# A kernel of two transformer blocks: the compression's weights move past its blocks, keys and values side by side, the gates' columns beside the first values'

## The chip, the cores and the metric

One core of one Trainium2 chip runs the whole program. The metric is device time in microseconds (us), as the median of three runs. Times in the trace are microseconds from the first instruction; the profiled execution is one execution by itself.

## The reference

Two blocks are computed on 512 tokens of width 1024 in f32. The change lies in the first one, in its mixer:

```python
h = rmsnorm(x, norm_mix_pre[i])
z = h @ w_in[i]
xr, gr, q, kc, vc, ksl, vsl, kw, vw, g_nsa, gm_rnn, gm_attn = jnp.split(z, IN_SPLITS, axis=-1)
...
kc_c = compress(kc.reshape(kv_shape), cmp_pos_k[i], cmp_k_w1[i], cmp_k_w2[i])
vc_c = compress(vc.reshape(kv_shape), cmp_pos_v[i], cmp_v_w1[i], cmp_v_w2[i])
y_attn = nsa(q, kc_c, vc_c, ksl..., vsl..., kw..., vw..., g_nsa, slopes)

def compress(kv, pos, w1, w2):          # kv: [1, 512, 4 groups, 64]
    c = kv.reshape(B, S // 16, 16, G, dh)
    blk = jnp.concatenate([c[:, :-1], c[:, 1:]], axis=2)   # 31 blocks of 32 tokens
    blk = blk + pos[:, None, :]
    blk = blk.transpose(0, 1, 3, 2, 4).reshape(B, nc, G, 32 * dh)   # 2048 wide
    return jax.nn.gelu(blk @ w1) @ w2    # w1: [2048, 256], w2: [256, 64]
```

`g_nsa` are 48 gate columns (16 heads by three branches) that go through a sigmoid; `vsl` and `vw` are 256 value columns each of the selected and the window branch. After the mixer come an output projection, a feed-forward stage, and a second block with a mixture of experts; none of that is touched.

## The kernel before

The program is written in a framework that records instructions with their data dependencies and then orders them by a planner of its own: each engine has one queue, in order, and the planner may put an instruction ahead of others that were written before it when their inputs are not there yet. Tiles come from pools; a tile waits until the earlier users of its buffer or its memory are done. So a pool's size and place decide when loads may start.

At the start the input x is normalised and transposed into `hh` and `hl` (`norm_hT`), the high and low part of h, 8 chunks of 128 channels by 512 tokens. A projection is three matmuls per chunk (`mm3`, lines 150 to 152: high by high, low by high, high by low). Its weights come through `win` and `wchunk`: `wload` (line 160) loads 8 x 128 rows into a tile `wr` of a ring of two buffers on SyncE's queue, then `split` (lines 155, 156) makes the high part `wh` on ACT and the low part `wl` on VectorE, 1024 columns of it at a time, in a ring of three buffers.

Then, in the order of the text: the gates (`gps`, lines 364 to 371): 24 matmuls of 512 tokens with 48 weight columns, a tanh on ACT, four transposes (`gpt`), one VectorE operation. The values `vsl` and `vw` (`vp`, line 380 copies them): for each of four groups of 128 tokens, 24 matmuls with h as the stationary side and 256 weight columns moving; two groups share one PSUM tile. Then `compress`, once for keys and once for values: the projection `kc` or `vc` (48 matmuls of 512 tokens, `pj`), 16 additions of the position vector on VectorE (line 446) that spread the projection over two tiles `E`, then the hidden layer `hp` (line 454): two halves of 128 hidden units, 16 matmuls each in plain f32, with a weight slice of `w1` as the stationary side and `E` read with a step of 8 elements as the moving side. Each f32 matmul stands as two records in the trace. The gelu (`gelu2`, lines 486 to 489) and the last product with `w2` (`kcp`, line 461, and `vcp`, line 474) follow. `w1` comes through the same ring `wr`, so two of its loads fill it until the hidden layer has read them.

Behind that the attention begins: `keys` projects 128 columns for each branch (`pj` again), then queries, pair by pair of heads, with the recurrence's projections in between.

Of the kernel before, what the change touches and what calls it, by code (L numbers as in the profile page):

```python
# [11 lines left out]
F32 = mybir.dt.float32  # L12
F32R = mybir.dt.float32r
# [3 lines left out]
AF = mybir.ActivationFunctionType  # L17
OP = mybir.AluOpType
# [4 lines left out]
OFF = dict(xr=0, gr=1024, q=2048, kc=3072, vc=3328, ksl=3584, vsl=3840, kw=4096, vw=4352, g=4608, gmr=4656, gma=5680)  # L23
# [82 lines left out]
class Kern:  # L106
# [228 lines left out]
    def mixer(self):  # L335
        nc, tc, a = self.nc, self.tc, self.a
        with ExitStack() as st:
            hp = st.enter_context(tc.tile_pool(name="hp", bufs=1))
            hh = hp.tile([128, 8, 512], F32R, name="hh")
            hl = hp.tile([128, 8, 512], F32R, name="hl")  # L340
            with tc.tile_pool(name="xp", bufs=1) as xp:
                x = xp.tile([128, 4, 1024], F32, name="x0")
                for i in range(4):
                    nc.sync.dma_start(x[:, i, :], a["x"][i * 128:(i + 1) * 128, :])
                self.vectors(0, nc.sync)
                self.norm_hT(xp, x, self.v["norm_mix_pre"], hh, hl, xp)
            self.hT = (hh, hl)
            self.dump("hh", hh.bitcast(F32))
            self.dump("hl", hl.bitcast(F32))
            kp = st.enter_context(tc.tile_pool(name="kp", bufs=1))  # L350
            dm = kp.tile([128, 512], F32, name="dm")
            nc.scalar.dma_start(dm, a["c_dm"])
            cmpd = kp.tile([128, 4, 32], F32, name="cmpd")
            nc.scalar.dma_start(cmpd, a["c_cmpd"])
            cmpm = kp.tile([128, 4, 32], F32, name="cmpm")
            nc.scalar.dma_start(cmpm, a["c_cmpm"])
            self.dm, self.cmpd, self.cmpm = dm, cmpd, cmpm
            self.vectors(1, nc.gpsimd)

            gw = self.win("g", 0, 48)  # L360
            gate = self.gate = kp.tile([128, 4, 48], F32, name="gate")
            ps = self.pp.tile([48, 512], F32, name="gps", tag="pp")
            for k in range(8):
                self.mm3(ps, gw[k], (hh[:, k, :], hl[:, k, :]), k == 0, k == 7)
            pt = self.pp.tile([128, 4, 48], F32, name="gpt", tag="pp")
            with tc.tile_pool(name="gtp", bufs=1) as gtp:
                gt = gtp.tile([48, 512], F32, name="gateT")
                nc.scalar.activation(gt, ps, AF.Tanh, scale=0.5)
                for i in range(4):
                    nc.tensor.transpose(pt[:, i, :], gt[:, i * 128:(i + 1) * 128], self.ident[0:48, 0:48])  # L370
            nc.vector.tensor_scalar(gate, pt, 0.25, 0.25, op0=OP.mult, op1=OP.add)
            self.V = {}
            for br in ("sl", "w"):
                w = self.win("v" + br)
                v = kp.tile([128, 4, 256], F32, name="v" + br)
                for i2 in range(2):
                    ps = self.pp.tile([128, 2, 256], F32, name=self.nm("vp"), tag="pp")
                    for i1 in range(2):
                        self.projtok(ps[:, i1, :], w, 2 * i2 + i1)
                    nc.vector.tensor_copy(v[:, 2 * i2:2 * i2 + 2, :], ps)  # L380
                self.V[br] = v
            self.KC, self.vcc = self.compress(kp)
            wk = self.wk = st.enter_context(tc.tile_pool(name="awork", bufs=2))
            self.rw = st.enter_context(tc.tile_pool(name="rwork", bufs=1))
            self.sp = st.enter_context(tc.tile_pool(name="sp", bufs=2, space=PSUM))
            self.op = st.enter_context(tc.tile_pool(name="op", bufs=1, space=PSUM))
            self.rnn_vectors()
            for c in range(4):
                if c % 2 == 0:
                    KD = self.keys(c // 2)  # L390
                w = self.win("q", c * 256)
                yA = []
                for m, ps in enumerate(self.proj(w)):
                    Q = []
                    for s in range(2):
                        q = wk.tile([128, 512], F32R, name=self.nm("qs"), tag="qs", bufs=4)
                        src = ps[s * 64:(s + 1) * 64, :]
                        nc.scalar.activation(q[0:64], src, AF.Copy, scale=0.125)
                        nc.vector.scalar_tensor_tensor(q[64:128], src, 0.125, q[0:64].bitcast(F32),
                                                       op0=OP.mult, op1=OP.subtract)  # L400
                        Q.append(q)
                    yA.append(self.pair(2 * c + m, Q, KD))
                self.rnn(c, yA)
# [19 lines left out]
    def compress(self, kp):  # L423

        nc, tc, a = self.nc, self.tc, self.a
        KC = (kp.tile([128, 4, 32], F32R, name="kch"), kp.tile([128, 4, 32], F32R, name="kcl"))
        vcc = kp.tile([64, 4, 64], F32, name="vcc")
        with tc.tile_pool(name="cmp", bufs=1) as cp, tc.tile_pool(name="cpp", bufs=2, space=PSUM) as cpp:
            for kv in ("k", "v"):
                w = self.win(kv + "c")  # L430
                w1 = []
                for e in range(2):
                    w1.append(self.wload(a[f"cmp_{kv}_w1"][e * 1024:(e + 1) * 1024], 8, 256))
                w2 = cp.tile([128, 2, 64], F32, name="cw2" + kv, tag="cw2")
                nc.scalar.dma_start(w2, a[f"cmp_{kv}_w2"].rearrange("(m p) h -> p m h", p=128))
                pos = self.v[f"cmp_pos_{kv}"]
                E = [cp.tile([128, 4, 256], F32, name=self.nm("E"), tag=f"E{e}") for e in range(2)]
                for m, ps in enumerate(self.proj(w)):
                    for s in range(2):
                        for par in range(2):  # L440
                            src = ps[s * 64:(s + 1) * 64, :].rearrange("p (u e) -> p u e", e=2)[:, :, par]
                            src = src.rearrange("p (n m) -> p n m", m=8)
                            for e in range(2):
                                pv = pos[par * 64:(par + 1) * 64, e * 8:(e + 1) * 8]
                                dst = E[e][par * 64:(par + 1) * 64, 2 * m + s, :].rearrange("p (n m) -> p n m", m=8)
                                nc.vector.tensor_tensor(dst, src, pv[:, None, :].to_broadcast([64, 32, 8]), op=OP.add)
                hid = cp.tile([128, 2, 4, 32], F32, name="hid" + kv, tag="hid")
                nc.vector.memset(hid, 0.0)
                for t in range(2):
                    ps = cpp.tile([128, 4, 31], F32, name=self.nm("hp"), tag="hp")  # L450
                    for m in range(16):
                        e, mm = divmod(m, 8)
                        rhs = E[e].rearrange("p g (n m) -> p g n m", m=8)[:, :, e:e + 31, mm]
                        nc.tensor.matmul(ps, w1[e][:, mm, t * 128:(t + 1) * 128], rhs, start=m == 0, stop=m == 15)
                    xs = cp.tile([128, 4, 31], F32, name=self.nm("gx"), tag="gx", bufs=2)
                    nc.scalar.activation(xs, ps, AF.Copy)
                    self.gelu2(hid[:, t, :, 0:31], xs, cp, [128, 4, 31], "gc")
                if kv == "k":
                    ps = cpp.tile([64, 128], F32, name="kcp", tag="hp")
                    for t in range(2):  # L460
                        nc.tensor.matmul(ps, w2[:, t, :], hid[:, t].rearrange("p g n -> p (g n)"), start=t == 0, stop=t == 1)
                    kh = KC[0].rearrange("p g n -> p (g n)")
                    kl = KC[1].rearrange("p g n -> p (g n)")
                    for s in range(2):
# [1 line left out]
                    for s in range(2):  # L466
                        nc.vector.scalar_tensor_tensor(kl[s * 64:(s + 1) * 64], ps, 0.5, kh[0:64].bitcast(F32),
                                                       op0=OP.mult, op1=OP.subtract)
                else:
                    ps = cpp.tile([64, 4, 64], F32, name="vcp", tag="hp")  # L470
                    for g in range(4):
                        for r in range(2):
                            for t in range(2):
                                nc.tensor.matmul(ps[r * 32:(r + 1) * 32, g, :], hid[:, t, g, :], w2[:, t, :],
                                                 start=t == 0, stop=t == 1)
                    nc.scalar.activation(vcc, ps, AF.Copy, scale=0.5)
        self.dump("kch", KC[0].bitcast(F32))
# [1569 lines left out]
```

## Time and profile before

| what | value |
|---|---|
| time, median of 3 runs | 2894.91 us (2894.25 to 2895.61) |
| profiled execution | 2891.96 us |
| its span, first to last instruction | 2890.2 us |
| mean granted clock of TensorE | 0.935 of 2.4 GHz |
| TensorE busy | 2541.2 us |
| VectorE busy | 1373.7 us |
| ACT busy | 863.2 us |
| POOL busy | 436.6 us |

The granted clock has two levels here, 1.00 (2.4 GHz) and 0.50 (1.2 GHz); a value between is a mean over a stretch. A row of the timeline shows its start, its length, the engine, the line, what is written and read, and in brackets how long the engine was idle before it and what ended that. Matmuls are pipelined, so the price of one is the distance of two starts, not the length of one.

### The profile page before, as it was taken

How to read it: one execution, taken by the hardware profiler on the slowest of the kernel's cores; microseconds unless marked ns; L12 is line 12 of the kernel's file. 1: busy time of each engine (PE TensorE's matmuls, PEld its weight loads, DVE VectorE, ACT ScalarE, POOL GpSimd, SP SyncE). 2: the span in 40 equal slices, each digit the busy share in tenths (PEclk: the TensorE clock that was granted, in tenths of full speed). 3: DMA queues.
4: the chain of work that ended last, by engine and by line, in shares of the span. 5: the costliest groups of instructions: out<-in, count | busy, mean ns of one | idle time of the engine just before them, and what ended most of it. 6: DMA issues, size and time to landing. Idle time of an engine off the chain costs nothing.

```text
span 2890.2 us, 44977 instructions
## 1 busy us (share of the span) xinstructions
PE 2541.2 (88%) x17137; PEld 1693.9 (59%) x17137; DVE 1373.7 (48%) x3625; ACT 863.2 (30%) x1764; POOL 436.6 (15%) x367
## 2 busy tenths in 40 slices
PE   7899999889999998897996999999868986968885
PEld 6767767677776776786776333333238775434442
DVE  4387787653333235686777221121167766101114
ACT  2265665532222123453541111110044431101111
POOL 1010010000010000011013231111030013512212
PEclk9899999999999998898997999999979997989998
DMA  3312111327777323242146899999831155999994
GB/s 122 105 43 61 58 44 59 104 99 230 234 234 236 107 86 101 81 146 71 45 152 224 352 392 419 426 427 427 321 128 63 35 189 222 406 425 421 399 392 162
DMA packets 228218, 595.74 MB, mean 206 GB/s; under 512 B 25109, under 2 KB 178265, under 8 KB 197025
## 3 DMA queue, kind: packets, MB, share of 16 engines
q1 hardware_dynamic: 200736, 552.81, 50.2%
q0 software_dynamic: 13888, 25.59, 2.4%
q10 hardware_dynamic: 13376, 14.43, 1.5%
q8 instruction: 138, 2.26, 0.3%
q14 instruction: 80, 0.65, 0.1%
HBM read 832.37 MB, written 25.92 MB: 297 GB/s over the span
## 4 chain that ended last, share of the span: by engine, by line
PE 64%; DMA 16%; DVE 13%; ACT 3%; issue 2%; POOL 0%; SPq 0%; ACTq 0%; POOLq 0%; DVEq 0%
DMA r<-w 14%; PE ph L1834 10%; PE pj L150 7%; PE pj L151 7%; PE pj L152 7%; PE py L1849 5%; PE tk L150 2%; PE oT L570 2%; PE tk L152 2%; PE ada L876 2%; PE tk L151 2%; PE dn L151 1%; PE dn L150 1%; PE dn L152 1%; PE tps L1821 1%
## 5 line engine op out<-in xcount | busy, mean ns | idle before, releaser
L1834 PE MATMUL ph<-r,xT 128*32 128x256 f32 (+1 forms) x4576 | 514.7, 461 | 62.2 <-DMA r<-w 59.7
L156 DVE TENSOR_TENSOR wl<-wr,wh 128x1024 fp32r<-128x1024 f32 (+1 forms) x193 | 236.9, 1232 | 311.2 <-ACT wh L155 308.7
L1834 PEld LDWEIGHTS ph<-r,xT 128*32 128x32 f32 (+1 forms) x4576 | 198.3, 122 | 314.3 <-issue 220.1
L155 ACT ACTIVATE wh<-wr 128x1024 fp32r<-128x1024 f32 (+1 forms) x193 | 202.8, 1055 | 427.2 <-PE pj L151 212.8
L1849 PE MATMUL py<-r,aT 128*32 128x256 f32 (+1 forms) x2288 | 253.5, 453 | 19.0 <-DMA r<-w 18.2
L1860 DVE SCALAR_TENSOR_TENSOR ys<-g2s,isc,g2s 128x512 f32<-128x512 f32 x41 | 44.2, 1082 | 303.8 <-DMA yd<-ys,dst 303.7
L1823 ACT ACTIVATE aT<-tps 128x128 f32<-128x128 f32 (+1 forms) x92 | 29.9, 324 | 516.4 <-PE tps L1821 516.4
L1849 PEld LDWEIGHTS py<-r,aT 128*32 128x32 f32 (+1 forms) x2288 | 92.4, 119 | 136.5 <-issue 91.4
L1841 DVE SCALAR_TENSOR_TENSOR et<-et,ph 128x128 f32<-128x128 f32 (+1 forms) x92 | 31.6, 343 | 292.2 <-ACT et L1840 292.2
L1815 POOL DMA_INDIRECT xg<-hxd,tok x92 | 96.3, 1046 | 410.8 <-PE tps L1821 379.3
L150 PE MATMUL pj<-hh,wh 128*128 128x512 f32 x384 | 154.4, 403 | 1.7 <-ACT wh L155 1.7
L151 PE MATMUL pj<-hl,wh 128*128 128x512 f32 x384 | 153.1, 399 | 0.0
L152 PE MATMUL pj<-hh,wl 128*128 128x512 f32 x384 | 152.3, 398 | 0.1
L150 PE MATMUL tk<-wh,lh 128*128 128x256 f32 x416 | 129.0, 310 | 17.4 <-DVE k2l L1173 8.0
L150 PE MATMUL pj<-h2h,wh 128*128 128x512 f32 x352 | 143.3, 407 | 0.1
L152 PE MATMUL pj<-h2h,wl 128*128 128x512 f32 x352 | 139.4, 396 | 0.0
L151 PE MATMUL pj<-h2l,wh 128*128 128x512 f32 x352 | 139.2, 395 | 0.0
L1862 POOL DMA_INDIRECT yd<-ys,dst x92 | 93.3, 1014 | 294.2 <-DVE ys L1861 274.5
L151 PE MATMUL tk<-wl,lh 128*128 128x256 f32 x416 | 125.4, 301 | 0.0
L152 PE MATMUL tk<-wh,ll 128*128 128x256 f32 x416 | 125.2, 301 | 0.0
L539 POOL TENSOR_SCALAR B<-dm 128x512 f32<-128x512 f32 x32 | 52.4, 1638 | 447.6 <-DVE z L554 257.0
L1410 POOL TENSOR_SCALAR s2r<-s2r 128x1024 f32<-128x1024 f32 x3 | 8.3, 2776 | 661.2 <-DMA s2r<-modd 661.2
(539 smaller groups left out, 5505.2 us busy)
## 6 DMA issues: line engine op xcount, KB each, us to landing
r<-w SPq DMA_DIRECT2D x194, 2048.0 KB
r<-w SPq DMA_DIRECT2D x192, 1024.0 KB
wr<-w_in SPq DMA_DIRECT2D x48, 1024.0 KB
adw<-w_ada SPq DMA_DIRECT2D x96, 512.0 KB
wr<-ffn_w_gate_up SPq DMA_DIRECT2D x22, 1024.0 KB
wr<-w_out SPq DMA_DIRECT2D x16, 1024.0 KB
wr<-ffn_w_down SPq DMA_DIRECT2D x10, 1024.0 KB
fy<-yd SPq DMA_DIRECT2D x10, 1024.0 KB
```

Of the source, the lines that this page charges most:

```text
L150: nc.tensor.matmul(out, sh, mh, start=start, stop=False)
L151: nc.tensor.matmul(out, sh, ml, start=False, stop=False)
L152: nc.tensor.matmul(out, sl, mh, start=False, stop=stop)
L155: self.nc.scalar.activation(hi, src, AF.Copy)
L156: self.nc.vector.tensor_tensor(lo, src, hi.bitcast(F32), op=OP.subtract)
L539: nc.gpsimd.tensor_scalar(B, dm, SLOPE[h], None, op0=OP.mult)
L570: nc.tensor.matmul(oT[s * 64:(s + 1) * 64, c * 128:512], V[br][:, c, g * 64:(g + 1) * 64], PT[s][:, c, c * 128:512], start=False, stop=las ...
L876: nc.tensor.matmul(ps[32 * j:32 * j + 32, h * 256:(h + 1) * 256], cs[:, k, :], w[:, j, :], start=k == 0, stop=k == 7, skip_group_check=True)
L1815: pin(nc.gpsimd.indirect_dma_start(xg[i % XG], None, hx, bass.IndirectOffsetOnAxis(tokc.bitcast(U32), 0), bounds_check=NT * 128 * ng - 1, ...
L1834: pin(nc.tensor.matmul(H[group(g)], X[:, k % nx, group(k // nx)], R13[s][n][:, q, :, cs], start=k == 0, stop=k == 7, skip_group_check=True))
L1849: pin(nc.tensor.matmul(Y[group(g)], A[:, k % na, group(k // na)], R2[s][n][:, q, g * CX:(g + 1) * CX], start=k == 0, stop=k == 3, skip_gro ...
L1862: d = nc.gpsimd.indirect_dma_start(yd, bass.IndirectOffsetOnAxis(dstc.bitcast(U32), 0), ys, None, bounds_check=NT * 256 * ng - 1, oob_is_e ...
```

## The change

Three things are edited. First, the gates lose their own projection: their 48 columns are loaded beside the 256 of the first values, into a pool `gwp` of their own on the right side of the memory (three tiles of 128 x 8 x 304), and the matmuls of these values move 304 columns instead of 256. Each group of 128 tokens has its own PSUM tile; ACT takes the tanh of the last 48 columns straight into `gate`. Second, in `compress` the blocks become the stationary side and the weights `w1` move past them: `E` is laid out as 8 x 4 x 32 so that the 128 blocks of one position lie side by side, a hidden layer is 16 matmuls of 256 columns into one tile, and its result, blocks by hidden units, is transposed after the gelu by two transposes and copied. Third, keys and values go side by side: both projections, then both hidden layers with their gelus, then both last products. `w1` gets four tiles of its own in the pool `cmp`, and `E`, `w2` and the gelu's tiles one for each side.

```diff
-            gw = self.win("g", 0, 48)
             gate = self.gate = kp.tile([128, 4, 48], F32, name="gate")
-            ps = self.pp.tile([48, 512], F32, name="gps", tag="pp")
-            for k in range(8):
-                self.mm3(ps, gw[k], (hh[:, k, :], hl[:, k, :]), k == 0, k == 7)
-            pt = self.pp.tile([128, 4, 48], F32, name="gpt", tag="pp")
-            with tc.tile_pool(name="gtp", bufs=1) as gtp:
-                gt = gtp.tile([48, 512], F32, name="gateT")
-                nc.scalar.activation(gt, ps, AF.Tanh, scale=0.5)
+            self.V = {}
+            gws = ExitStack()
+            gwp = gws.enter_context(tc.tile_pool(name="gwp", bufs=1, side="right"))
+            for br in ("sl", "w"):
+                n = 304 if br == "sl" else 256
+                if n > 256:
+                    raw = gwp.tile([128, 8, n], F32, name="vgw")
+                    for o, c in (("v" + br, slice(0, 256)), ("g", slice(256, n))):
+                        src = a["w_in"][:, OFF[o]:OFF[o] + c.stop - c.start]
+                        nc.sync.dma_start(raw[:, :, c], src.rearrange("(k p) c -> p k c", p=128))
+                    hi = gwp.tile([128, 8, n], F32R, name="vgh")
+                    lo = gwp.tile([128, 8, n], F32R, name="vgl")
+                    for k in range(0, 8, 4):
+                        self.split(hi[:, k:k + 4], lo[:, k:k + 4], raw[:, k:k + 4])
+                    w = [(hi[:, k], lo[:, k]) for k in range(8)]
+                else:
+                    w = self.win("v" + br)
+                v = kp.tile([128, 4, 256], F32, name="v" + br)
                 for i in range(4):
-                    nc.tensor.transpose(pt[:, i, :], gt[:, i * 128:(i + 1) * 128], self.ident[0:48, 0:48])
-            nc.vector.tensor_scalar(gate, pt, 0.25, 0.25, op0=OP.mult, op1=OP.add)
-            self.V = {}
-            for br in ("sl", "w"):
-                w = self.win("v" + br)
-                v = kp.tile([128, 4, 256], F32, name="v" + br)
-                for i2 in range(2):
-                    ps = self.pp.tile([128, 2, 256], F32, name=self.nm("vp"), tag="pp")
-                    for i1 in range(2):
-                        self.projtok(ps[:, i1, :], w, 2 * i2 + i1)
-                    nc.vector.tensor_copy(v[:, 2 * i2:2 * i2 + 2, :], ps)
+                    ps = self.pp.tile([128, n], F32, name=self.nm("vp"), tag="pp")
+                    self.projtok(ps, w, i)
+                    nc.vector.tensor_copy(v[:, i, :], ps[:, 0:256])
+                    if n > 256:
+                        nc.scalar.activation(gate[:, i, :], ps[:, 256:304], AF.Tanh, scale=0.5)
                 self.V[br] = v
+            nc.vector.tensor_scalar(gate, gate, 0.25, 0.25, op0=OP.mult, op1=OP.add)
+            gws.close()
...
+            w1, w2, E = {}, {}, {}
             for kv in ("k", "v"):
                 w = self.win(kv + "c")
-                w1 = []
+                w1[kv] = [cp.tile([128, 8, 256], F32, name=f"cw1{kv}{e}") for e in range(2)]
                 for e in range(2):
-                    w1.append(self.wload(a[f"cmp_{kv}_w1"][e * 1024:(e + 1) * 1024], 8, 256))
+                    nc.sync.dma_start(w1[kv][e], a[f"cmp_{kv}_w1"][e * 1024:(e + 1) * 1024].rearrange("(k p) c -> p k c", p=128))
...
+                E[kv] = [cp.tile([128, 8, 4, 32], F32, name=f"E{kv}{e}") for e in range(2)]
+                nc.gpsimd.memset(E[kv][1][:, :, :, 31:32], 0.0)
...
-                            src = src.rearrange("p (n m) -> p n m", m=8)
+                            src = src.rearrange("p (n m) -> p m n", m=8)
...
-                                dst = E[e][par * 64:(par + 1) * 64, 2 * m + s, :].rearrange("p (n m) -> p n m", m=8)
-                                nc.vector.tensor_tensor(dst, src, pv[:, None, :].to_broadcast([64, 32, 8]), op=OP.add)
...
+                                dst = E[kv][e][par * 64:(par + 1) * 64, :, 2 * m + s, 0:32 - e]
+                                nc.vector.tensor_tensor(dst, src[:, :, e:], pv[:, :, None].to_broadcast([64, 8, 32 - e]), op=OP.add)
+            G = {}
+            for kv in ("k", "v"):
+                ps = cpp.tile([128, 256], F32, name="hp" + kv, tag="hp")
+                for m in range(16):
+                    e, mm = divmod(m, 8)
+                    nc.tensor.matmul(ps, E[kv][e][:, mm].rearrange("p g n -> p (g n)"), w1[kv][e][:, mm, :], start=m == 0, stop=m == 15)
+                xs = cp.tile([128, 256], F32, name="gx" + kv)
+                nc.scalar.activation(xs, ps, AF.Copy)
+                self.gelu2(xs, xs, cp, [128, 256], "gc" + kv)
+                G[kv] = xs
+            for kv in ("k", "v"):
+                ps = cpp.tile([128, 2, 128], F32, name="ht" + kv, tag="hp")
                 for t in range(2):
-                    ps = cpp.tile([128, 4, 31], F32, name=self.nm("hp"), tag="hp")
-                    for m in range(16):
-                        e, mm = divmod(m, 8)
-                        rhs = E[e].rearrange("p g (n m) -> p g n m", m=8)[:, :, e:e + 31, mm]
-                        nc.tensor.matmul(ps, w1[e][:, mm, t * 128:(t + 1) * 128], rhs, start=m == 0, stop=m == 15)
...
+                    nc.tensor.transpose(ps[:, t, :], G[kv][:, t * 128:(t + 1) * 128], self.ident)
+                hid = cp.tile([128, 2, 128], F32, name="hid" + kv)
+                nc.vector.tensor_copy(hid, ps)
...
```

## Rows read from the trace of the kernel before

**Rows 1.** The page, first part: busy time, share of the span, instructions.

```profile
PE 2541.2 (88%) x17137; PEld 1693.9 (59%) x17137; DVE 1373.7 (48%) x3625; ACT 863.2 (30%) x1764; POOL 436.6 (15%) x367
```

**Rows 2.** Windows: stretch, its length, engines' busy time, clock, DMA share, GB/s.

```profile
24.35:123.37 99.02, 86.69 (x480) 75.73 (x481) 32.82 (x90) 11.75 (x22) 0.01 (x1) 0.90 0.26 80
123.37:145.70 22.33, 22.20 (x99) 17.97 (x97) 14.12 (x16) 11.50 (x16) 3.49 (x2) 1.00 0.55 171
145.70:250.00 104.30, 101.79 (x494) 72.18 (x493) 83.57 (x247) 65.28 (x135) 13.04 (x8) 1.00 0.17 54
```

**Rows 3.** Timeline of TensorE, gates and first values.

```profile
24.35 0.43 PE L150 MATMUL gps<-hh,wh 128*48 128x512 f32 x1 [0.87 <-DVE hl L270]
...
31.55 0.45 PE L370 MATMUL gpt<-ident,gateT 48*128 48x48 f32 x4 [1.45 <-ACT gateT L368]
31.93 0.39 PE L150 MATMUL vp<-wh,hh 128*128 128x256 f32 x1
...
36.04 0.28 PE L150 MATMUL vp<-wh,hh 128*128 128x256 f32 x1
...
39.98 0.28 PE L150 MATMUL vp<-wh,hh 128*128 128x256 f32 x1
```

**Rows 4.** Timeline of TensorE, compression of keys and then values.

```profile
56.55 0.40 PE L150 MATMUL pj<-hh,wh 128*128 128x512 f32 x1
...
67.22 0.39 PE L152 MATMUL pj<-hh,wl 128*128 128x512 f32 x1
...
70.80 14.81 PE L454 MATMUL hp<-E,wr 128*128 128x124 f32 x64 [3.19 <-DVE E L446]
85.55 0.43 PE L461 MATMUL kcp<-hidk,cw2k 128*64 128x128 f32 x2
87.30 0.69 PE L461 MATMUL kcp<-hidk,cw2k 128*64 128x128 f32 x2 [1.32 <-DVE hidk L489]
89.71 0.79 PE L150 MATMUL pj<-hh,wh 128*128 128x512 f32 x1 [1.72 <-ACT wh L155]
...
105.97 14.70 PE L454 MATMUL hp<-E,wr 128*128 128x124 f32 x64 [3.19 <-DVE E L446]
120.60 0.30 PE L474 MATMUL vcp<-cw2v,hidv 128*32 128x64 f32 x2
122.35 1.09 PE L474 MATMUL vcp<-cw2v,hidv 128*32 128x64 f32 x30 [1.46 <-DVE hidv L489]
123.37 0.50 PE L150 MATMUL pj<-hh,wh 128*128 128x512 f32 x1
```

**Rows 5.** Waits of SyncE's queue, 24 to 125 us: total, times, longest.

```profile
SPq L160 <- PE hp L454: 51.7, 3, 24.6
SPq L160 <- DVE wl L156: 47.3, 5, 19.4
```

**Rows 6.** Windows behind two waits; the clock is third from the end.

```profile
31.90:38.00 6.10, 6.10 (x40) 6.07 (x39) 1.92 (x8) 0.00 (x0) 0.00 (x0) 0.72 0.06 13
...
89.70:93.70 4.00, 3.99 (x9) 3.14 (x10) 2.35 (x2) 0.90 (x1) 0.00 (x0) 0.50 0.35 84
```

**Rows 7.** Windows of the hidden layer alone: PE, PEld, ACT, clock, DMA.

```profile
71.00:76.00 5.00, 5.00 (x23) 5.00 (x24) 0.00 (x0) 0.50 0.02 3
77.00:85.00 8.00, 8.00 (x38) 7.40 (x37) 0.27 (x1) 1.00 0.22 63
```

**Rows 8.** Timeline of TensorE elsewhere: plain f32 matmuls.

```profile
1276.66 0.98 PE L1458 MATMUL lgp<-wg,hxT 128*128 128x36 f32 x8
...
200.25 1.02 PE L652 MATMUL px<-xc,bdx 128*128 128x512 f32 x2
```

**Rows 9.** Tile px: durations min/median/max in ns, first and last start.

```profile
L652 PE MATMUL px<-xc,bdx x16: 592/592/593, 197.2 to 521.5; 128*128 128x512 f32 x16
```

**Rows 10.** Tile E: the position adds, durations min/median/max in ns.

```profile
L446 DVE TENSOR_TENSOR E<-pj,vec x32: 405/419/428, 64.9 to 105.8; 64x256 f32<-64x256 f32 x32
```

**Rows 11.** Tile gu: one gelu step elsewhere, ns min/median/max.

```profile
L487 DVE SCALAR_TENSOR_TENSOR gu<-gu,g x28: 415/426/694, 189.5 to 2267.0; 128x256 f32<-128x256 f32 x20, 128x512 f32<-128x512 f32 x8
```

More of the change, by code (lines that the diff above doesn't have):

```diff
@@ L428, in compress @@
         with tc.tile_pool(name="cmp", bufs=1) as cp, tc.tile_pool(name="cpp", bufs=2, space=PSUM) as cpp:
+            w1, w2, E = {}, {}, {}
             for kv in ("k", "v"):
                 w = self.win(kv + "c")
-                w1 = []
+                w1[kv] = [cp.tile([128, 8, 256], F32, name=f"cw1{kv}{e}") for e in range(2)]
                 for e in range(2):
-                    w1.append(self.wload(a[f"cmp_{kv}_w1"][e * 1024:(e + 1) * 1024], 8, 256))
-                w2 = cp.tile([128, 2, 64], F32, name="cw2" + kv, tag="cw2")
-                nc.scalar.dma_start(w2, a[f"cmp_{kv}_w2"].rearrange("(m p) h -> p m h", p=128))
+                    nc.sync.dma_start(w1[kv][e], a[f"cmp_{kv}_w1"][e * 1024:(e + 1) * 1024].rearrange("(k p) c -> p k c", p=128))
+                w2[kv] = cp.tile([128, 2, 64], F32, name="cw2" + kv)
+                nc.scalar.dma_start(w2[kv], a[f"cmp_{kv}_w2"].rearrange("(m p) h -> p m h", p=128))
                 pos = self.v[f"cmp_pos_{kv}"]
-                E = [cp.tile([128, 4, 256], F32, name=self.nm("E"), tag=f"E{e}") for e in range(2)]
+                E[kv] = [cp.tile([128, 8, 4, 32], F32, name=f"E{kv}{e}") for e in range(2)]
+                nc.gpsimd.memset(E[kv][1][:, :, :, 31:32], 0.0)
                 for m, ps in enumerate(self.proj(w)):
@@ L447, in compress @@
-                hid = cp.tile([128, 2, 4, 32], F32, name="hid" + kv, tag="hid")
-                nc.vector.memset(hid, 0.0)
-                for t in range(2):
-                    ps = cpp.tile([128, 4, 31], F32, name=self.nm("hp"), tag="hp")
-                    for m in range(16):
-                        e, mm = divmod(m, 8)
-                        rhs = E[e].rearrange("p g (n m) -> p g n m", m=8)[:, :, e:e + 31, mm]
-                        nc.tensor.matmul(ps, w1[e][:, mm, t * 128:(t + 1) * 128], rhs, start=m == 0, stop=m == 15)
-                    xs = cp.tile([128, 4, 31], F32, name=self.nm("gx"), tag="gx", bufs=2)
-                    nc.scalar.activation(xs, ps, AF.Copy)
-                    self.gelu2(hid[:, t, :, 0:31], xs, cp, [128, 4, 31], "gc")
+                                dst = E[kv][e][par * 64:(par + 1) * 64, :, 2 * m + s, 0:32 - e]
@@ L460, in compress @@
                     for t in range(2):
-                        nc.tensor.matmul(ps, w2[:, t, :], hid[:, t].rearrange("p g n -> p (g n)"), start=t == 0, stop=t == 1)
+                        nc.tensor.matmul(ps, w2[kv][:, t, :], hid[:, t], start=t == 0, stop=t == 1)
                     kh = KC[0].rearrange("p g n -> p (g n)")
@@ L473, in compress @@
                             for t in range(2):
-                                nc.tensor.matmul(ps[r * 32:(r + 1) * 32, g, :], hid[:, t, g, :], w2[:, t, :],
+                                nc.tensor.matmul(ps[r * 32:(r + 1) * 32, g, :], hid[:, t, g * 32:(g + 1) * 32], w2[kv][:, t, :],
                                                  start=t == 0, stop=t == 1)
```

## The prediction

> **What bounds the kernel now.** I read the page first: TensorE is busy for 88% of the span [rows 1], so time is to be won where TensorE stands or works slowly. The edit touches one stretch, between the first normalisation and the first key projections of the attention. By windows that stretch runs from 24.35 us (first gate matmul) to 123.37 us (first matmul of the key projections), 99.02 us at a mean granted clock of 0.90, with the DMA engines at 0.26 and VectorE at a third [rows 2]. So neither transfers nor VectorE bound it as a whole. What follows has TensorE busy for 22.20 of 22.33 us and then 101.79 of 104.30 us per quarter of the attention [rows 2]: work released earlier there simply starts earlier. I therefore take a microsecond won in the stretch as one won at the end.
>
> Then I read TensorE's timeline through the stretch, start by start. Gates with their tail: 24.35 to 31.93, 7.6 us [rows 3]. Values: 31.93 to 56.55, 24.6 us [rows 3, 4]. Keys' projection and the wait behind it: to 70.80, 14.3; keys' hidden layer (hp): to 85.55, 14.7; its tail and the wait for the next weights: to 89.71, 4.2; values' projection and wait: to 105.97, 16.3; their hp: to 120.60, 14.6; their tail: to 123.37, 2.8 [rows 4]. The sum is 99.0. Inside it the reader should see four waits, marked in brackets: twice 3.19 us for the position adds, 1.32 and 1.46 us for the gelu, and 1.72 us for a weight split [rows 4]. Behind a wait the clock falls to its lower level: it is 0.72 over 31.9 to 38.0, after the gate's tail, and 0.50 over 89.7 to 93.7 [rows 6].
>
> **Gates.** Removed: 24 matmuls of 512 columns, the wait for the tanh (1.45 us), four small transposes; 7.6 us go. Added: 48 columns to each of the 96 matmuls of the first values. At the full clock 256 columns start every (39.98-36.04)/33 = 0.120 us [rows 3], 512 columns every (67.22-56.55)/47 = 0.227 us [rows 4]: 0.107/256 us per column, so 304 columns take 0.140 and the 96 take 13.4 us; the second values 96 x 0.120 = 11.5 us. The two together are 24.9 against 24.6 before, where the first 4 us ran below the full clock; that loss goes because no wait stands ahead of them any more. The first matmul now needs the split of 4 x 304 columns where it needed the gate's 384 in all, and that split shares ACT and VectorE with the normalisation: it may start 0.5 us earlier (less other work there) to 2.5 us later (both halves late). I take 0.5 us later. The four tanh of 48 columns and four copies lie behind 3.4 us of matmuls each, with three PSUM buffers; without that cover they would cost under 1 us in all. The vector constants of the recurrence may move behind these values, if their memory is what the new 29 KB pool takes; VectorE is idle there for two thirds, and their readers come 100 us later.
>
> **Projections side by side.** 48 matmuls each at 0.227: 21.8 us for both. The keys' 16 adds take 0.42 us each [rows 10]; half run before their projection ends, and 3.19 us stand exposed each time [rows 4]. Now the keys' adds lie under the values' projection (10.9 us) and the values' under the keys' hp. Both 3.19 us waits go, and with them the half-clock stretches behind. The adds now read PSUM at steps of 16 elements instead of 2, and no row shows that step. From 0.42 us each they may grow to 0.68 before the keys' adds come out from under 10.9 us; up to there it costs nothing.
>
> **Hidden layer.** Before, 32 matmuls a side, 64 records (each f32 matmul shows as two) of 124 moving columns read at steps of 8 elements: (14.81-0.40)/63 = 0.229 us a record [rows 4]. After, 16 matmuls, 32 records of 256 adjacent columns. The price is not in the trace, so I bound it. At the full clock f32 records of 512 adjacent columns with the same 128-column weights start (1.02-0.592) = 0.43 us apart; of 36 columns (0.98-0.28)/7 = 0.10 us apart [rows 8, 9] (0.28 taken as the last one's own length). By columns, 256 cost 0.215. Upper end: today's 0.229. I take 0.215, since 512 columns at 128-column weights is the nearest shape: 64 x 0.215 = 13.8 us for both sides against 29.3.
>
> One oddity supports it: hp passes 23 records in 5 us at clock 0.50 and 38 in 8 us at 1.00 [rows 7], the same pace, while 36 columns pass at 0.10. So at the full clock neither array nor weight load sets the pace, and the strided read is what is left. The Trainium skill (SBUF — State Buffer, section on the DMA port swizzle) says SBUF has 16-byte lines and an access that changes line each time pays; a 32-byte step does so. The trace agrees as far as those rows go.
>
> **Tails.** The work itself: transposes of the gelu's result about 0.5, the keys' last product 0.7, the values' 1.1 us, 2.3 together. Exposed at most: gelu of the values on 256 columns, five steps near 0.42 [rows 11] with gaps 2.3, transposes 0.35, copy 0.43, last product 1.1, 4.2 us (the keys' own tail fits inside). The lower end holds if key projections of the attention fill the wait. I take 3.2, the middle, since their weights can be there (next paragraph), but before nothing filled the 1.46 us wait.
>
> **Transfers.** The four 1 MB weight loads of hp leave the ring of two buffers and get four own ones (the work area grows by some 40 KB, to about 55). SyncE's queue waited 51.7 us for hp and 47.3 us for splits [rows 5]: the first kind goes. The new tiles lie where the normalisation's input was, so their loads start after 24 us. If they stood ahead of the second values' weights in the queue, those would come up to 6 us late. Same bytes: 80 GB/s over 99 us [rows 2] become 124 over 64; the stretch behind it moves 171 [rows 2]. I cost it at nothing. ACT's two small loads move with it; nothing waits behind them. POOL gets two small memsets, with TensorE 40 us away from needing them.
>
> **Sum.** 0.5 + 13.4 + 11.5 + 21.8 + 13.8 + 3.2 = 64.2 us in place of 99.0: 34.8 us less. The profiled execution took 1.8 us more than its span, 2891.96 us; less 34.8 it is 2857.2. The median stands 2.95 above the profiled execution: 2860.
>
> **Rivals.**
> A, hp does not get cheaper. Either the weight load stands serially before each matmul, or the columns keep today's price. First: 0.10 + 0.215 = 0.32 a record, 20.5 us, 2867. Second: 256 x 0.229/124 = 0.47 a record, 30.3 us, 2877. Against the first: 256 columns at 128-column weights start every 0.120 us [rows 3], with no room for a load between. The Trainium skill (TensorE: Matmul & The Clock Gate, Part 3) says that weight loads overlap running matmuls only on different row groups, which would give this first form; the 0.120 us contradict it here. Chance 0.07.
> B, a new wait takes part of it back: the second values' weights or a split late, or VectorE's order puts the constants or splits ahead of adds, and the clock falls behind it as it did over 89.7 to 93.7 (each fall cost about 2 us: 9 records [rows 6] in 4 us that hold 17.6 at 0.227). Two or three such waits, 7 to 15 us: 2867 to 2875. For it: three buffers of split weights are shared by three projections. Chance 0.14.
> C, slower: the adds with their 16-element step. The first add can start near 57.9 (one half-projection of 2.7 us before the keys' projection ends), the values' hp and tail take 11.1 us behind the last of 32; so they decide from (123.4-57.9-11.1)/32 = 1.7 us each. At 2.0 us the key projections of the attention begin at 133, 10 us later than before: 2905. Against it: the 2-element step costs 0.42 us for 256 elements [rows 10], as much as 256 adjacent ones in SBUF, 0.43 [rows 11]. Chance 0.03.
> D, no change: what is won is waited for later. It would take a stage tied to transfers from the start; at 0.17 of DMA in the attention [rows 2] there is none near. Chance 0.03.
>
> **Numbers.** The forecast keeps 0.73. Its own range: start -1 to +2, hp +0.9, tail -0.9 to +1, the changed interleaving later 4 us either way: 2853 to 2868. With most of A and B: 2852 to 2874, leaving out B's and A's ends, C and D and some of the forecast's own tail, under 0.2. Faster by over 0.2% (5.8 us, about what a measurement tells from no change) 0.94, same 0.03, slower 0.03.
>
> **What would show it.** After: no gps; first vp near 24.9 and no low clock behind it; 304-column matmuls 0.14 apart; the two projections without a gap; hp 64 records in all, 0.215 apart, at clock 1.00; no wait on E; first key projections near 88.5. Wrong if hp stays above 0.3 a record, if SyncE or a split holds a projection, or if the adds pass 0.68 us.

## The result and the profile after

The changed kernel takes 2855.72 us (median of 4, 2853.89 to 2858.52), the kernel before 2895.26 beside it (median of 4): ratio 0.986, 95% interval 0.9847 to 0.9873. That is 39.5 us less; 34.8 were forecast, and 2855.72 lies in the range of 2852 to 2874. A repeat further down gave 37.9 us. The two profiled executions, 2891.96 and 2858.52 us, lie 33.4 apart. The trace settles what of these numbers belongs to the change.

The timeline of TensorE after the change, from the first value matmul to the first matmul of the attention's compressed scores (c):

```profile
24.24 0.62 PE L150 MATMUL vp<-vgh,hh 128*128 128x304 f32 x1
...
38.76 0.28 PE L150 MATMUL vp<-wh,hh 128*128 128x256 f32 x1
...
50.27 0.40 PE L150 MATMUL pj<-hh,wh 128*128 128x512 f32 x1
...
72.06 7.07 PE L461 MATMUL hpk<-cw1k,Ek 128*128 128x256 f32 x32
78.96 7.07 PE L461 MATMUL hpv<-cw1v,Ev 128*128 128x256 f32 x32
85.87 0.38 PE L469 MATMUL htk<-ident,gxk 128*128 128x128 f32 x2
86.01 0.48 PE L150 MATMUL pj<-hh,wh 128*128 128x512 f32 x1
...
86.88 0.65 PE L475 MATMUL kcp<-hidk,cw2k 128*64 128x128 f32 x4
...
88.49 0.38 PE L469 MATMUL htv<-ident,gxv 128*128 128x128 f32 x2
...
89.51 1.11 PE L488 MATMUL vcp<-cw2v,hidv 128*32 128x64 f32 x32
...
110.18 0.39 PE L516 MATMUL c<-qs,kch 128*32 128x512 f32 x1
```

No row bears a bracket: none of the waits of [rows 4] is left. Both projections run as one block from 50.27 to 72.06, both hidden layers as another to 85.87, and the tails of the compression stand among the attention's key projections (pj at 86.01, between htk and kcp). The windows say the same in sums:

```profile
24.24:26.50 2.26, 2.26 (x9) 2.26 (x10) 2.26 (x4) 1.64 (x3) 0.65 (x3) 0.51 0.29 72
26.50:38.76 12.26, 12.26 (x89) 12.26 (x88) 4.57 (x6) 1.88 (x5) 0.00 (x0) 1.00 1.10 348
24.24:110.20 85.96, 85.96 (x489) 75.69 (x490) 48.31 (x113) 22.55 (x37) 5.70 (x8) 0.99 0.44 130
```

TensorE is busy for 85.96 of 85.96 us at a mean clock of 0.99. Before, the row over the part up to the key projections has 86.69 of 99.02 us at 0.90 [rows 2].

**One measure for all runs.** From the first matmul on h to c it is 121.35 us before and 85.94 after: 35.4 less. This distance is called the stretch from here on. A second trace of each kernel gives 121.3 and 86.5, which is 34.8 less. The table splits the stretch of every trace at the first matmul of the keys' projection (the first pj); all columns are distances of starts, in us. The front holds the gates and the values.

| kernel | front: first matmul on h to first pj | first pj to c | stretch |
|---|---|---|---|
| before | 32.2 | 89.15 | 121.35 |
| before, second trace | 32.2 | 89.1 | 121.3 |
| gates' columns alone | 26.6 | 89.6 | 116.2 |
| matmuls turned round alone | 31.3 | 75.6 | 106.9 |
| side by side alone | 34.0 | 74.7 | 108.7 |
| layout alone | 33.8 | 78.7 | 112.5 |
| after | 26.0 | 59.9 | 85.9 |
| after, second trace | 26.6 | 59.9 | 86.5 |
| after, one side after the other | 27.3 | 60.5 | 87.7 |
| after, weights stationary | 26.1 | 60.1 | 86.2 |
| after, weights in the ring | 25.0 | 77.9 | 102.9 |

From the first pj to c the two pairs of equal kernels agree to 0.1 us. The front scatters more: from 31.3 to 34.0 where its text is that of the kernel before, and from 25.0 to 27.3 where it is the changed one. So a difference of a microsecond or two in the whole stretch can come from a front that an experiment did not touch, and the middle column is the better judge of what it did behind it.

Behind c the eleven traces of this study need between 2742.0 and 2755.0 us, in no order by kernel: before 2744.5 and 2755.0, after 2746.5 and 2742.0. Counted from c, every matmul up to 380 us behind it stands at the same place in all eleven traces, to 0.7 us; the scatter comes later. So the change is worth 35 us in its stretch, and the distance of two medians holds the scatter behind it as well. The order of the instructions behind the stretch is the same before and after on the five engines of the page.

### The profile page after: what moved, and what is told of

Its sections match the earlier page's. It is cut to its first block, busy times and chain, and to the rows that moved or that the text cites. A ratio compares the mean times of both kernels' runs of the same rounds, so it can differ in the third digit from the quotient of the medians.

```text
span 2856.7 us, 44802 instructions
## 1 busy us (share of the span) xinstructions
PE 2518.9 (88%) x17049; PEld 1673.4 (59%) x17049; DVE 1369.7 (48%) x3624; ACT 863.0 (30%) x1760; POOL 436.7 (15%) x369
## 4 chain that ended last, share of the span: by engine, by line
PE 65%; DMA 16%; DVE 13%; ACT 3%; issue 2%; SPq 0%; POOL 0%; ACTq 0%; POOLq 0%; DVEq 0%
DMA r<-w 14%; PE ph L1848 10%; PE pj L150 7%; PE pj L151 7%; PE pj L152 7%; PE py L1863 5%; PE tk L150 2%; PE oT L584 2%; PE tk L152 2%; PE tk L151 2%; PE ada L890 2%; PE dn L150 1%; PE dn L151 1%; PE dn L152 1%; PE tps L1835 1%
## 5 line engine op out<-in xcount | busy, mean ns | idle before, releaser
L1848 PE MATMUL ph<-r,xT 128*32 128x256 f32 (+1 forms) x4576 | 515.8, 463 | 63.2 <-DMA r<-w 60.5
L156 DVE TENSOR_TENSOR wl<-wr,wh 128x1024 fp32r<-128x1024 f32 x190 | 233.6, 1234 | 306.7 <-ACT wh L155 304.1
L155 ACT ACTIVATE wh<-wr 128x1024 fp32r<-128x1024 f32 x190 | 200.2, 1058 | 419.3 <-PE pj L151 234.2
L1863 PE MATMUL py<-r,aT 128*32 128x256 f32 (+1 forms) x2288 | 252.6, 451 | 16.8 <-DMA r<-w 16.0
L1874 DVE SCALAR_TENSOR_TENSOR ys<-g2s,isc,g2s 128x512 f32<-128x512 f32 x41 | 36.7, 898 | 301.4 <-DMA yd<-ys,dst 301.4
```

The source lines that it names most:

```text
L155: self.nc.scalar.activation(hi, src, AF.Copy)
L156: self.nc.vector.tensor_tensor(lo, src, hi.bitcast(F32), op=OP.subtract)
L1848: pin(nc.tensor.matmul(H[group(g)], X[:, k % nx, group(k // nx)], R13[s][n][:, q, :, cs], start=k == 0, stop=k == 7, skip_group_check=True))
L1863: pin(nc.tensor.matmul(Y[group(g)], A[:, k % na, group(k // na)], R2[s][n][:, q, g * CX:(g + 1) * CX], start=k == 0, stop=k == 3, skip_gro ...
```

## The experiments

**Each part alone, on the kernel before.** Four kernels shared one chip and 17 runs of the kernel before (median 2897.53 us).

The gates' columns alone:

```diff
-            gw = self.win("g", 0, 48)
...
+                n = 304 if br == "sl" else 256
...
+                        nc.scalar.activation(gate[:, i, :], ps[:, 256:304], AF.Tanh, scale=0.5)
```

> The kernel before with the gates' part of the change alone. My sum: the gates' 7.6 us go, the 96 wider matmuls cost 0.02 us each more (1.9), the slow clock over the first values (about 1.7 us) goes: 7.4 us faster, near 2888. Rival (the gates were cover for weights that are late): the first or second values then wait for their split, a vp row with a wait by ACT or VectorE appears, and under 3 us are won.

Measured: 2890.86 us, 6.7 less, ratio 0.998 (0.9971 to 0.999); the stretch is 116.2 us, 5.1 less than 121.3. No row of vp waits for its weights, so the rival is out. The sum was 2.3 above what the stretch shows, and 1.7 of that is the slow clock, which does not go; it moves to the front, and the wide matmuls take 15.1 us, not 13.4:

```profile
24.20:28.30 4.10, 4.10 (x19) 4.10 (x20) 3.47 (x5) 2.77 (x4) 0.49 (x1) 0.59 0.41 112
28.30:38.30 10.00, 10.00 (x73) 10.00 (x73) 3.54 (x5) 0.64 (x3) 0.00 (x0) 1.00 0.37 113
```

The granted clock is 0.59 over the first 4.1 us of the wide matmuls. TensorE had stood 1.3 us for VectorE (hl) before the last transposes, and 0.4 us before the first wide matmul.

The hidden layer's matmuls turned round alone, one side after the other, weights through the ring. The blocks are laid adjacent too, since the turned form reads them so:

```diff
-                        rhs = E[e].rearrange("p g (n m) -> p g n m", m=8)[:, :, e:e + 31, mm]
-                        nc.tensor.matmul(ps, w1[e][:, mm, t * 128:(t + 1) * 128], rhs, start=m == 0, stop=m == 15)
...
+                    nc.tensor.matmul(ps, E[e][:, mm].rearrange("p g n -> p (g n)"), w1[e][:, mm, :], start=m == 0, stop=m == 15)
```

> The kernel before with the hidden layer's matmuls turned round alone (blocks stationary, weights of 256 columns moving), one side after the other, weights through the ring of two. My sum: 0.215 us a record at the full clock, but 0.43 behind the wait for the adds while the clock is low (before, some 5.6 us of each hidden layer): 13 + 19 records, about 9.7 us a side against 14.7, less 1.5 us a side for a longer tail (gelu on 256 columns, transposes, copy): 6 to 8 us faster in all. Rival (turning round is worth its full 7.8 us a side by itself): 13 to 16 us faster. Rival (price goes by columns): no gain.

Measured: 2880.70 us, 16.8 less, ratio 0.9937 (0.992 to 0.9954); the stretch is 106.9, 14.4 less. My 6 to 8 us were wrong. Two windows of the keys' hidden layer, and one of the values' projection behind it:

```profile
72.00:74.00 2.00, 2.00 (x6) 1.56 (x5) 0.00 (x0) 0.00 (x0) 0.00 (x0) 0.50 0.00 0
74.00:76.00 2.00, 2.00 (x10) 1.77 (x10) 0.00 (x0) 0.00 (x0) 0.00 (x0) 1.00 0.00 0
...
82.17:97.00 14.83, 11.96 (x52) 9.26 (x52) 8.45 (x20) 1.44 (x3) 0.00 (x0) 1.00 0.36 119
```

The wait for the adds is still there (3.13 us), but the low clock behind it ends near 74; before it was 0.50 from 71 to 76 [rows 7]. And the values' projection starts in the shade of the keys' tail at clock 1.00, where it ran at 0.50 before [rows 6]. The hidden layers take 8.9 and 8.8 us, not 9.7, against 14.8 and 14.7 before: 11.8 less for both. From the first pj to c it is 13.5 less. So the longer tail, which I had priced at 3 us, cost nothing in sum, since the values' projection fills part of the keys' tail. The first rival has the number, 13 to 16, but not for its reason: a side became 5.9 us cheaper, not 7.8.

Keys and values side by side alone, with four weight tiles of their own:

```diff
+                w1[kv] = [cp.tile([128, 8, 256], F32, name=f"cw1{kv}{e}") for e in range(2)]
...
+            for kv in ("k", "v"):
+                hid = G[kv] = cp.tile([128, 2, 4, 32], F32, name="hid" + kv)
...
+                        rhs = E[kv][e].rearrange("p g (n m) -> p g n m", m=8)[:, :, e:e + 31, mm]
```

> The kernel before with keys and values side by side and the compression's weights in four tiles of their own, gates and the matmuls of the hidden layer as before (weights stationary, blocks read at steps of 8). My sum: both waits for adds (6.4 us), the wait for the split (1.7), the keys' tail (2.7) and the values' wait (1.5) go, and the clock no longer falls (about 2 us at the values' projection): 13 to 15 us faster; hp stays at 0.226 to 0.229 us a record at clock 1.00. Rival (waits move elsewhere): under 8 us, with a wait row before pj or hp.

Measured: 2878.60 us, 18.9 less, ratio 0.9934 (0.992 to 0.9948); the stretch is 108.7, 12.6 less. From the first pj to c it is 14.4 less, inside the 13 to 15 forecast; the front, which this edit leaves alone, took 1.8 us more. Both waits for adds, the wait for the split and the gelu's waits are gone. What is left of TensorE's waits between the first matmul on h and c:

```profile
PE gpt L370 <- ACT gateT L368: 1.4, 1, 1.4
PE gps L150 <- DVE hl L270: 0.6, 1, 0.6
```

The strided hidden layer keeps its price at the full clock throughout:

```profile
81.20:95.50 14.30, 14.30 (x65) 13.22 (x65) 5.43 (x13) 1.95 (x4) 0.00 (x0) 1.00 0.13 40
```

65 records in 14.3 us are 0.22 each. So the old form is as slow at 1.00 as it was over the low stretch.

The layout of the blocks alone, weights stationary as before:

```diff
-                E = [cp.tile([128, 4, 256], F32, name=self.nm("E"), tag=f"E{e}") for e in range(2)]
+                E = [cp.tile([128, 8, 4, 32], F32, name=self.nm("E"), tag=f"E{e}") for e in range(2)]
...
-                        rhs = E[e].rearrange("p g (n m) -> p g n m", m=8)[:, :, e:e + 31, mm]
+                        rhs = E[e][:, mm, :, 0:31]
```

> The kernel before with the layout of the blocks alone: the 31 blocks of a position adjacent in memory, weights stationary as before, 124 columns moving. If the step of 8 elements set the pace (my reading): 0.11 to 0.12 us a record at the full clock, still 0.215 at the low one, so each hidden layer falls from 14.7 to about 10 us, 9 to 10 us faster in all. If it was a floor of plain f32 matmuls with 128 weight columns (rival): 0.226 a record stays, no change.

Measured: 2886.47 us, 11.1 less, ratio 0.996 (0.9946 to 0.9974); the stretch is 112.5, 8.8 less; from the first pj to c it is 10.4 less, where 9 to 10 were forecast.

```profile
72.37 9.04 PE L454 MATMUL hp<-E,wr 128*128 128x124 f32 x64 [3.13 <-DVE E L446]
```

```profile
74.00:76.00 2.00, 2.00 (x13) 2.00 (x11) 0.00 (x0) 0.00 (x0) 0.00 (x0) 0.54 0.00 0
78.00:80.00 2.00, 2.00 (x20) 2.00 (x19) 0.58 (x2) 0.76 (x3) 0.00 (x0) 1.00 0.00 0
```

The same 64 records take 9.0 us where they took 14.8 [rows 4]; their pace follows the clock now (13 against 20 in 2 us), which it did not do before [rows 7]. The shapes and the order of these matmuls are those of before, and only the step of the moving read is another, so the step set the pace. The rule of the Trainium skill (SBUF — State Buffer, section on the DMA port swizzle) that a read pays when each access changes its 16-byte line agrees with this pair.

The stretches of the three parts of the change alone sum to 5.1 + 14.4 + 12.6 = 32.1 us; together they give 35.4. The front's scatter is in both numbers.

**What of the order, the matmul's form and the buffers does it.** Three kernels on one chip, beside 11 runs of the kernel before (median 2895.71 us).

The changed kernel with keys and values written one after the other again, own weight tiles kept:

```diff
-            G = {}
-            for kv in ("k", "v"):
                 ps = cpp.tile([128, 256], F32, name="hp" + kv, tag="hp")
...
-            for kv in ("k", "v"):
                 ps = cpp.tile([128, 2, 128], F32, name="ht" + kv, tag="hp")
```

> The changed kernel, written one side after the other again (keys: projection, hidden layer, last product; then values), with the four weight tiles of their own kept. Theory one, the order of the text matters: the waits for the adds (two of about 3.2 us) and the clock's falls behind them come back, 8 to 12 us slower than the changed kernel, 2864 to 2868. Theory two, the buffers matter and the planner fills the waits by itself once the values' weights are there: within 2 us of the changed kernel, no wait for E over 1 us.

Measured: 2857.47 us, ratio to before 0.9871 (0.9856 to 0.9885); the stretch is 87.7 us, no wait of TensorE in it.

```profile
65.79 7.09 PE L459 MATMUL hpk<-cw1k,Ek 128*128 128x256 f32 x32
75.17 0.44 PE L466 MATMUL htk<-ident,gxk 128*128 128x128 f32 x2
76.24 0.65 PE L472 MATMUL kcp<-hidk,cw2k 128*64 128x128 f32 x4
84.89 7.09 PE L459 MATMUL hpv<-cw1v,Ev 128*128 128x256 f32 x32
```

The first hidden layer starts at 65.79 instead of 72.06: the planner put part of the values' projection ahead of it, and the rest behind. Theory two holds: once the buffers are there, the order of the text hardly matters. Of the 1.8 us by which the stretch is longer than after, 1.2 lie in the front; from the first pj to c the order costs 0.5 us.

The changed kernel with weights stationary and adjacent blocks moving:

```diff
-                    nc.tensor.matmul(ps, E[kv][e][:, mm].rearrange("p g n -> p (g n)"), w1[kv][e][:, mm, :], start=m == 0, stop=m == 15)
+                        nc.tensor.matmul(ps, w1[kv][e][:, mm, t * 128:(t + 1) * 128], E[kv][e][:, mm, :, 0:31], start=m == 0, stop=m == 15)
...
-                    nc.tensor.transpose(ps[:, t, :], G[kv][:, t * 128:(t + 1) * 128], self.ident)
```

> The changed kernel with weights stationary again and adjacent blocks of 124 columns moving (no transposes, no copy of the hidden layer). If a record of 124 adjacent columns takes 0.11 to 0.12 us, 128 records take 14 to 15 us against 13.8 and the time is within 2 us of the changed kernel: then turning the matmul round is worth no more than laying the blocks adjacent. If it stays at 0.226, 29 us against 13.8: 15 us slower, near 2871.

Measured: 2857.06 us, ratio 0.9866 (0.9851 to 0.9882); the stretch is 86.2 us.

```profile
71.57 7.30 PE L464 MATMUL hp<-Ek,cw1k 128*128 128x124 f32 x64
78.71 7.31 PE L464 MATMUL hp<-Ev,cw1v 128*128 128x124 f32 x64
```

(7.30 - 0.27)/63 = 0.112 us a record, 0.27 being one record's length: 14.4 us for both sides, against 13.8 with the weights moving. By these prices turning the matmul round is worth half a microsecond over laying the blocks side by side; from the first pj to c the two kernels are 0.2 us apart (60.1 and 59.9).

The changed kernel with the compression's weights back in the ring of two:

```diff
-                w1[kv] = [cp.tile([128, 8, 256], F32, name=f"cw1{kv}{e}") for e in range(2)]
-                for e in range(2):
-                    nc.sync.dma_start(w1[kv][e], ...)
+                w1[kv] = [self.wload(a[f"cmp_{kv}_w1"][e * 1024:(e + 1) * 1024], 8, 256) for e in range(2)]
```

> The changed kernel with the four weight loads of the compression put back into the ring of two buffers. Theory (own tiles remove the waits): the values' weights come only when the keys' hidden layer has read its own; waits for a split or a load return in front of the values' projection and hidden layer, the clock falls, 8 to 15 us slower than the changed kernel, near 2866. Rival (transfers were covered anyway, the order alone did it): within 2 us.

Measured: 2871.52 us, ratio 0.9918 (0.9902 to 0.9934), 15.8 above the first median of the changed kernel and just above the 8 to 15 that were forecast; the stretch is 102.9 us. The three longest waits of TensorE:

```profile
PE hpv L459 <- DVE Ev L453: 3.1, 1, 3.1
PE hpk L459 <- DVE Ek L453: 3.1, 1, 3.1
PE pj L150 <- ACT wh L155: 3.0, 1, 3.0
```

and the waits of SyncE's queue for the hidden layers:

```profile
SPq L160 <- PE hpk L459: 20.8, 2, 17.8
SPq L160 <- PE hpv L459: 20.1, 1, 20.1
```

The text is side by side, yet all three waits are back, since the values' weights cannot be loaded while the keys' fill the ring. So 17.0 of the 35.4 us hang on four tiles of memory; from the first pj to c it is 18.0 of 29.2, since the front of this run was a quick one.

**The scatter.** Both kernels unaltered, beside 17 further runs of the kernel before (median 2893.92 us).

> The changed kernel once more, unaltered. By the traces the attention starts 35.5 us earlier, while the first medians lay 39.5 us apart. If the 4 us between are the scatter of executions behind that point, this comparison gives anything from 34 to 40 us and the median of nine profiled executions behind the attention's start is the same for both kernels; if they are real, it gives 39 to 40 again.

Measured: 2855.99 us, 37.9 less, ratio 0.9868 (0.9848 to 0.9888, which is 32 to 44 us); the stretch is 86.5. That lies in the 34 to 40 of the first case and does not repeat the 39 to 40 of the second, but its interval allows both. Nine profiled executions of each kernel were not taken, so the question is not settled by this run.

> The kernel before as if it were a change: no difference, and its interval shows what a comparison can tell here; I expect plus or minus 3 us. In its profile the first matmul of the attention's compressed scores stands at 145.7 us again, to 0.5 us.

Measured: 2895.86 us against 2893.92, ratio 1.0004 (0.9993 to 1.0015), which is from 2 us less to 4 us more, about as expected; c stands at 146.5, not within 0.5 us of 145.7, because the first matmul on h is 0.9 us later too. The kernel before runs from 2889.60 to 2903.25 us here, and its profiled execution, with a stretch of 121.3 us, took 2903.25: of the 11.3 us over the first one, 10.5 lie behind c.

## Why the prediction was right

**What bounds it.** That the stretch was TensorE's alone, with waits and a low clock in it, held: 85.96 of 85.96 us are busy now, and all that was released arrives at the attention and is still there 380 us behind c.

**Gates.** Right in sign, with two sizes off. Start: half a microsecond later was forecast, it is 0.1 earlier (24.24 for 24.35 [rows 3]). The 96 wide matmuls were put at 13.4 us; they take 14.5 (24.24 to 38.76). Their price at the full clock was right: (38.62-26.72)/85 = 0.140 us between the rows at 26.72 and 38.62.

```profile
26.72 0.30 PE L151 MATMUL vp<-vgl,hh 128*128 128x304 f32 x1
...
38.62 0.30 PE L152 MATMUL vp<-vgh,hl 128*128 128x304 f32 x1
```

The step that failed is "that loss goes because no wait stands ahead of them any more": TensorE waits 1.8 us for VectorE before the last transposes, and the first matmuls, nine in the window up to 26.50, run at 0.51. The row of its waits (total, times, longest):

```profile
PE tp L268 <- DVE hl L270: 2.1, 2, 1.8
```

Such a wait does not always bring the low clock. In the run with the weights in the ring, TensorE stands the same 1.8 us before the same transposes, and yet the clock is 1.00 throughout and the 96 matmuls take 13.5 us, next to the 13.4 forecast:

```profile
22.64 0.66 PE L268 MATMUL tp<-ident,xn 128*128 128x128 f32 x4 [1.78 <-DVE hl L270]
23.95:37.49 13.54, 13.54 (x97) 13.54 (x97) 6.77 (x9) 3.44 (x7) 0.58 (x1) 1.00 0.40 122
```

In the other five traces with this edit they take 14.5 to 15.8 us, each with a part at 0.50. The second values, forecast at 11.5, take 11.5.

**Projections and adds.** 21.8 us forecast, 50.27 to 72.06 measured. The adds at a step of 16 elements of PSUM cost what they did at 2:

```profile
58.66 6.11 DVE L455 TENSOR_TENSOR Ek<-pj,vec 64x256 f32<-64x256 f32 x16 [0.57 <-PE pj L152]
```

16 in 6.11 us end at 64.77, 7 us before the keys' hidden layer needs them. Rival C is out.

**Hidden layer.** 13.8 us forecast, 72.06 to 85.87 measured, 0.215 us a record. Rival A is out in both forms: a load in front of each matmul would have made it 20.5 us, and 0.112 us at 124 adjacent columns leaves no room for one either. There the Trainium skill (TensorE: Matmul & The Clock Gate, Part 3) and the trace differ, where it says that weight loads overlap running matmuls only when the row groups differ: these loads are all on the same ones, and there is no room for them outside the matmuls. The same Part names a background weight buffer as a second case in which a load goes ahead; no run here tells whether that is it. The remark that the strided read was what was left was right, and the layout alone showed it.

**Tails.** 3.2 us was the middle of 2.3 and 4.2. From 85.87 to 110.18 are 24.3 us. The 96 key and query matmuls in it took 22.3 before, from 123.37 to c [rows 2]; 2.0 remain, just under the lower end: the key projections do fill the gelu's waits.

**Transfers.** Costed at nothing, and nothing is what they cost. SyncE's queue:

```profile
24.05 0.99 SPq L440 DMA_DIRECT2D cw1k<-cmp_k_w  x2
30.47 0.37 SPq L160 DMA_DIRECT2D wr<-w_in  x1
30.90 5.21 SPq L440 DMA_DIRECT2D cw1v<-cmp_v_w  x2
```

The loads wait for the normalisation's memory, as expected, and the values' projection weights leave at 30.47, some 20 us before the first split that reads them. The terms sum to -0.1 + 14.5 + 11.5 + 21.8 + 13.8 + 2.0 = 63.5 us; 64.2 was forecast. That these two lie so close is partly luck: the wide matmuls took 1.1 us more, the start 0.6 and the tails 1.2 us less, and the three nearly cancel. The large terms, projections and hidden layer, were right by themselves.

**Rivals B and D.** No wait took anything back, and what came behind the stretch passed it on. The forecast time itself is 4.3 us above the first median: the step that failed is "the median stands 2.95 above the profiled execution". It moved the kernel's own scatter, seen in three runs, onto another kernel; the changed kernel's median stands 2.8 below its profiled execution. Over 17 runs the kernel before spreads by 13 us.

Whether its median behind c is really some microseconds above that of the changed kernel stays open. The medians lean that way: in all four comparisons, of the changed kernel twice and of its two variants with the buffers kept, they fell by 3 to 5 us more than the stretch did (39.5, 38.2, 38.7 and 37.9 us, against 35.4, 33.6, 35.2 and 34.8), and the first interval, 36.8 to 44.3 us, leaves 35.4 out. The traces, two of each kernel, do not show it.

## What to carry to other kernels

When an engine waits in a stretch where transfers and the other engines are idle, ask first which buffer holds the next load back: here four tiles of memory brought 17 of 35 us, and the order of the text half a microsecond once they were there. Look at the step of every moving operand before turning a matmul round: adjacent columns cost 0.112 us per 124 with the weights stationary and 0.104 with them moving, against 0.23 at a step of 8. And judge a small change by a marker inside the traces when the rest of the kernel scatters by more than the change.

## What the runs showed that was not expected

The clock behind one and the same wait does not come back after the same time, and the form of the matmuls does not decide it. Before, after the wait of 3.19 us, the strided matmuls of the keys ran at 0.50 from 71 to 76 us [rows 7]. After the same wait the strided matmuls of the values, which start at 105.97, are back at 1.00 from 111 us:

```profile
108.00:110.00 2.00, 2.00 (x11) 2.00 (x10) 0.00 (x0) 0.00 (x0) 0.00 (x0) 0.50 0.00 0
111.00:115.00 4.00, 4.00 (x19) 3.70 (x18) 0.50 (x2) 0.89 (x3) 0.00 (x0) 1.00 0.01 4
```

The turned matmuls show both as well: alone, the keys' were back at 1.00 from 74 us, after a start at 70.37; with the weights in the ring, the values', which start at 91.10 behind a wait of 3.1 us, are still at 0.50 up to 96 us:

```profile
92.00:96.00 4.00, 4.00 (x11) 3.10 (x11) 0.00 (x0) 0.00 (x0) 0.00 (x0) 0.50 0.00 0
97.00:101.00 4.00, 4.00 (x21) 3.46 (x20) 0.00 (x0) 0.00 (x0) 0.00 (x0) 1.00 0.48 131
```

What decides it was not tried. So what a low clock costs behind one wait does not carry over to the next place: my 6 to 8 us for the turned matmuls came from the keys' stretch of the kernel before.

And a strided plain f32 matmul runs at one pace, 0.21 to 0.22 us per 124 columns, at either clock (23 records in 5 us at 0.50 and 38 in 8 us at 1.00 [rows 7]), so a low clock costs nothing there.
